# Attention stepped twice as often between projections, six output projections in two pieces, and a conditional whose short side comes first

## The chip, the cores and the metric

The kernel runs on one core of a Trainium2 chip. The metric is the device time of one execution in microseconds, the median of several runs. PE is TensorE, DVE VectorE, ACT ScalarE, POOL GpSimd and SP the engine that issues most DMAs. The names in the order lists below are those of the program (`bank_67` is one of eight PSUM banks).

## What is computed

Two blocks in float32 on 256 tokens of width 1024. The first adds 16 meta tokens and has a pool mixer, a gated linear attention and a hierarchical mixture of 16 experts. The second has two layers, each with a feed-forward part, an attention and another feed-forward part, modulated by a condition. Its stream x (256 tokens) is attended together with a context of 256 tokens; the last layer computes the context only as far as x needs it. One layer of the second block, cut to its core:

```python
u = modulate(rms_norm(h))                 # x and context, per stream
q, k, v = split(u @ w_in)                 # 16 heads of 64
a = window_attention(q_a, k_a, v_a)       # 6 heads, with a sink per head
b = global_attention(rms(q_b), rms(k_b), v_b)   # 4 heads
c = neighbourhood_attention(q_c, k_c, v_c)      # 6 heads, with a bias
h = h + gate * (concat(a, b, c) @ w_out)
```

The mixture of experts has for each token a group (of 4) and two experts in it:

```python
h = silu(xt @ w_gate[e]) * (xt @ w_up[e])
y = y + combine[:, e:e + 1] * (h @ w_down[e])
```

## The kernel before

Every product of two float32 matrices is made from three: each operand is split into a high part (a cast, ACT, "hi") and the rest (a subtraction, DVE, "lo"), and PE multiplies hi by hi, hi by lo and lo by hi. A weight tile of 128 by 1024 comes by DMA into `raw`, ACT makes `hi`, DVE makes `lo`. Tokens stand in the free dimension: x in columns 0 to 255, context in 256 to 511.

One program is written out in Python, and what stands behind what on an engine is decided while it is written. `Program.work(cols)` is called behind each group of matmuls of a projection and counts their columns. At 3000 (`unit`) it calls `tick()`: that prepares the next weight tile (`pump`) and advances every background generator in `bg` by one step. Three matmuls of 512 columns are 1536 columns, so a tick comes every 6 of them (every 12 of 256). The norms, the tails of the projections (rotary embedding, norms of q and k) and the attention of the second block are such generators.

`mix(l)` is the attention part of layer l. Its projections are units in the order of `mix_units(l)`: q and k tiles ("q", 0 to 12; 0 to 7 are queries, 8 to 12 keys), the values of windows and global heads ("vwg", two pieces, `v_units`), the values of the neighbourhood ("vc", four pieces). `attention()` works on items: for each of 8 head pairs two row tiles of x (16 items "x") and, in layer 0, one of the context (8 items "c"). An item may begin when what stands in its `need` is in `have`, until now the query tile, the key tile and the values. One turn of its loop handles three items at different stages, with a `yield` between the stages:

- `t_out` of the item before last: ACT casts the transposed probabilities (`ptH`), DVE makes the rest (`ptL`);
- `exps` (ACT) and `sums` (DVE: sums, reciprocals) of the item before;
- `scores` of a new item (PE, L875), then `maxes` (DVE);
- `v_out` (ACT, DVE) and `values` (PE, L968; L975 broadcasts the reciprocals to all rows);
- `transposes` of the item before (PE, L936).

The generator is started behind the projection "vwg" (`self.start(att)` in `mix`), and advanced by ticks alone. When the projections have run out while items are left, `until` and `drain` advance it with nothing in between.

The output projection has 8 tiles of rows. `OUT2` is ((0, 5), (5, 3)): the first `NO` tiles are made in two pieces, k-tiles 0 to 4 as soon as these heads are done, 5 to 7 later; each piece ends in its own residual addition on DVE (`residual`: h = h + gate * bank). The others are made whole. In layer 0 the last four units of that list (`NW`) run through `run_halves`: first all four on the context's columns, then all four on x; when the context half is done, `after(1)` starts the context's norm for the next feed-forward part, which is advanced by the ticks of the x half. The norm: a sum of squares on PE (L449), a power on POOL, a broadcast on PE (L453), products (DVE, `tmp<-h,modT,bank`), casts (ACT, `uH`), rests (DVE, `uL`). The next part begins with the context's columns.

In the first block, experts have a fixed number of places; a flag (`over`) says whether a second pass is needed. `more_places` loads the flag (L1727) and wraps this pass in `tc.If(rv > 0)` (L1730), which in these runs isn't taken. Its body has 662 instructions on PE, 244 on DVE, 252 on ACT. If it isn't taken, each engine still has to add to its semaphores what the body would have added, in an else side that is placed behind the body; there an engine waits for its own work first.

Small tiles: `small` holds 6 of 128 by 16 for norms, and `sums` 6 of 128 by 16 for the items' maxima, sums and reciprocals.

## Time and profile before

| | us |
|---|---|
| median of 3 runs | 2073.07 (2070.8 to 2075.65) |
| the profiled execution, its own time | 2073.52 |
| its span in the profile | 2071.7 |
| PE busy | 2016.8 (97%) |
| DVE busy | 1406.7 (68%) |
| ACT busy | 818.8 (40%) |

Layer 0's attention part ends at about 946 us, layer 1's at about 1866; the conditional is at 296 to 305 us. A row of the timeline gives the start, the duration, engine, line, operation, output and inputs, sizes and the number of instructions, and in brackets how long the engine was idle before it and what released it. The duration of a matmul row runs past the start of the next one, since matmuls are pipelined; the time that it costs PE is read from start to start.

### The profile page before, as it was taken

What the parts mean: (1) busy time and instruction counts of PE and PEld (TensorE: products, weight loads), DVE (VectorE), ACT (ScalarE), POOL (GpSimd) and SP (SyncE); (2) the same over time, 40 slices, a digit from 0 to 9 for tenths busy, and PEclk for the clock granted to TensorE, in tenths of its full rate; (3) what the DMA queues carried; (4) which work ended last, traced back from release to release, by engine and by line L of the source; (5) the groups of instructions that cost most, each with busy time, mean ns of one, the idle gap of its engine ahead of it and who ended that gap; (6) DMA issues with size and microseconds to landing.
All of it is one profiled execution on the core that took longest, in us unless ns stands there. A gap on an engine that the chain in (4) does not pass through costs nothing.

```text
span 2071.7 us, 30268 instructions
## 1 busy us (share of the span) xinstructions
PE 2016.8 (97%) x11972; PEld 1753.5 (85%) x11972; DVE 1406.7 (68%) x2344; ACT 818.8 (40%) x1404; POOL 64.0 (3%) x87
## 2 busy tenths in 40 slices
PE   7999989999999999999999999999999999999998
PEld 7977769888888988789888888988888899889998
DVE  6888876787763656667886744778665365667554
ACT  5357654222222455555312222432222245555442
POOL 1200000000000100000000000000000010000000
PEclk9999999999999999999999999999999999999999
DMA  6669973565540311025655533365543122137551
GB/s 229 202 241 353 360 258 122 183 203 193 189 126 21 101 57 43 29 89 184 212 186 193 168 109 110 106 210 186 167 164 123 52 68 87 49 105 256 184 175 48
DMA packets 92598, 318.11 MB, mean 154 GB/s; under 512 B 11616, under 2 KB 14976, under 8 KB 92064
## 3 DMA queue, kind: packets, MB, share of 16 engines
q1 hardware_dynamic: 88496, 306.75, 44.5%
q0 software_dynamic: 2624, 9.08, 1.3%
q8 instruction: 96, 1.57, 0.3%
q10 hardware_dynamic: 1328, 0.27, 0.1%
q14 instruction: 54, 0.44, 0.1%
HBM read 315.01 MB, written 1.05 MB: 153 GB/s over the span
## 4 chain that ended last, share of the span: by engine, by line
PE 69%; issue 12%; DVE 3%; ACT 1%; DMA 0%; POOL 0%; POOLq 0%; DVEq 0%; ACTq 0%
PE bank L352 61%; PE bank L968 2%; PE bank L830 2%; PE bank L875 1%; PE bank L936 1%; DVE tmp L130 1%; PE bank L975 1%; ACT probs L912 0%; DVE uL L130 0%; DMA bias<-in_bias_dram 0%; DVE lo L130 0%; ACT ptH L701 0%; PE bank L1785 0%; DVE ptL L130 0%; PE bank L453 0%
## 5 line engine op out<-in xcount | busy, mean ns | idle before, releaser
L352 PE MATMUL bank<-uH,hi 128*128 128x512 f32 (+2 forms) x888 | 301.5, 345 | 7.9 <-DVEq L1730 6.4
L352 PE MATMUL bank<-uH,lo 128*128 128x512 f32 (+2 forms) x888 | 297.7, 341 | 1.5 <-DVE lo L130 1.5
L352 PE MATMUL bank<-uH,xhi 128*128 128x512 f32 (+2 forms) x832 | 285.2, 344 | 2.0 <-ACT uH L1162 2.0
L352 PE MATMUL bank<-uH,xlo 128*128 128x512 f32 (+2 forms) x832 | 283.9, 343 | 0.0
L352 PE MATMUL bank<-uL,hi 128*128 128x512 f32 (+2 forms) x888 | 282.4, 340 | 0.0
L352 PE MATMUL bank<-uL,xhi 128*128 128x512 f32 (+2 forms) x832 | 278.6, 342 | 0.0
L130 DVE CUSTOM_DVE_ANT_0 tmp<-xraw,cs,vec 128x1024 bf16<-128x1024 f32 x192 | 245.8, 1281 | 3.4
L352 PEld LDWEIGHTS bank<-uH,hi 128*128 128x128 f32 x888 | 170.6, 192 | 30.6 <-DVEq L1730 6.9
L352 PEld LDWEIGHTS bank<-uH,lo 128*128 128x128 f32 x888 | 170.6, 192 | 20.0 <-DVE lo L130 1.9
L604 ACT CAST hidH<-tmp 128x512 fp32r<-128x512 f32 (+1 forms) x97 | 51.6, 532 | 335.6 <-DVE tmp L130 335.5
L352 PEld LDWEIGHTS bank<-uH,xhi 128*128 128x128 f32 x832 | 157.8, 190 | 22.6 <-ACT uH L1162 2.4
L352 PEld LDWEIGHTS bank<-uL,hi 128*128 128x128 f32 x888 | 161.4, 191 | 17.1
L352 PEld LDWEIGHTS bank<-uH,xlo 128*128 128x128 f32 x832 | 157.7, 190 | 19.5
L352 PEld LDWEIGHTS bank<-uL,xhi 128*128 128x128 f32 x832 | 154.9, 189 | 19.3
L130 DVE SCALAR_TENSOR_TENSOR h<-bank,modT,h 128x256 f32<-128x256 f32 x204 | 92.8, 480 | 112.9 <-PE bank L352 112.7
L130 DVE TENSOR_TENSOR lo<-raw,hi 128x1024 fp32r<-128x1024 f32 (+3 forms) x111 | 123.7, 1120 | 39.6 <-ACT hi L257 37.9
L130 DVE TENSOR_TENSOR xlo<-xraw,xhi 128x1024 fp32r<-128x1024 f32 (+1 forms) x97 | 115.2, 1189 | 48.7 <-ACT xhi L257 48.5
L595 ACT ACTIVATE tmp<-bank 128x512 f32<-128x512 f32 (+1 forms) x97 | 49.5, 510 | 234.4 <-PE bank L352 232.6
L130 DVE TENSOR_TENSOR tmp<-tmp,bank 128x512 f32<-128x512 f32 (+1 forms) x97 | 55.9, 577 | 126.9 <-PE bank L352 126.2
L130 DVE TENSOR_TENSOR lo<-xraw,hi 128x1024 fp32r<-128x1024 f32 (+1 forms) x96 | 114.9, 1202 | 37.9 <-ACT hi L257 37.5
L352 PE MATMUL bank<-hidH,xhi 128*128 128x512 f32 (+1 forms) x400 | 134.7, 337 | 0.0
L352 PE MATMUL bank<-hidH,xlo 128*128 128x512 f32 (+1 forms) x400 | 134.5, 336 | 0.0
(427 smaller groups left out, 4437.1 us busy)
## 6 DMA issues: line engine op xcount, KB each, us to landing
xraw<-in_w_ada_dram SPq DMA_DIRECT2D x96, 512.0 KB, 3.5
xraw<-in_w_ffn_up_dram SPq DMA_DIRECT2D x52, 512.0 KB, 4.2
xraw<-in_w_ffn_gate_dram SPq DMA_DIRECT2D x50, 512.0 KB, 3.7
raw<-in_w_ada_dram SPq DMA_DIRECT2D x48, 512.0 KB, 4.3
xraw<-in_w_expert_gu_dram SPq DMA_DIRECT2D x43, 512.0 KB, 5.8
raw<-in_w_ffn_gate_dram SPq DMA_DIRECT2D x38, 512.0 KB, 4.3
raw<-in_w_ffn_up_dram SPq DMA_DIRECT2D x36, 512.0 KB, 3.7
xraw<-in_w_ffn_down_dram SPq DMA_DIRECT2D x32, 512.0 KB, 4.0
```

The lines of the kernel that those rows point to most:

```text
L130: return f(*args, **kw)
L352: nc.tensor.matmul(o, a(k), b[:, k, cols], start=start and k == ks[0] and j == 0, stop=stop and k == ks[-1] and j == len(prods) - 1, skip_ ...
L595: nc.scalar.activation(t[:, :cols.stop - cols.start], u.bank[:, cols], AF.Silu)
L604: nc.scalar.copy(H, tt)
L830: nc.tensor.matmul(b, x[:, kk, tok], y(k), start=first, stop=a == ws - 1 and k == per - 1 and j == 2, skip_group_check=True)
L875: nc.tensor.matmul(it["S"][j][:, o], a[rows, i, q], b[rows, kt, kk], start=n == 0 and o.start == 0, stop=n == 2, skip_group_check=True)
L936: nc.tensor.transpose(b[:, o * P:(o + 1) * P], src, self.ident)
L968: nc.tensor.matmul(b[:n, X], a[:, k + dk, v0:v0 + n], p[:, k, :], start=j == 0 and k == ks[0], stop=j == 2 and k == ks[-1], skip_group_che ...
L975: nc.tensor.matmul(b[64 * j:64 * j + 64, 256 + a * P:256 + (a + 1) * P], rs.to_broadcast([P, 64]), self.ident, start=True, stop=True, skip ...
```

## The change

1. `work` advances one generator, the attention (`fast`), also when 1500 columns (`FU`) have been counted since it last moved. With three matmuls of 512 it now moves behind every three, with those of 256 behind every six; all other generators still move at ticks.
2. The attention is started in front of the projection "vwg" instead of behind it. The items of the first five head pairs no longer need "vwg" to begin; `values` yields until it is there. In layer 1 the units 1 and 9 move ahead of "vwg", and 5 behind "vc".
3. `NO` is (6, 6) instead of (4, 4).
4. Maxima and sums use the tiles of `small` (8 now), put back right behind `sums`; the reciprocals go to slices of a new tile `recs`.
5. The flag is loaded ahead of the last expert's down projection, and the conditional gets `preferred_fallthrough_block=False`.

```diff
-NO = (4, 4)
+NO = (6, 6)
+FU = 1500
@@ work
         self.cols += cols
+        self.fast_cols += cols
         if self.cols >= self.unit:
             self.tick()
+        elif self.fast_cols >= FU and self.fast in self.bg:
+            self.fast_cols = 0
+            self.step(self.fast)
@@ mix_units
-        return q(8, 10, 11, 12, 0) + vwg + q(1, 2, 9, 3, 4, 5) + vc + q(6, 7)
+        return q(8, 10, 11, 12, 0, 1, 9) + vwg + q(2, 3, 4) + vc + q(5, 6, 7)
@@ attention
-            st = it["st"] = self.sums.get()
+            st = it["st"] = self.small.get()
...
+            it["rec"] = self.recs.get()
...
-            self.v.reciprocal(st[:, 4:4 + n], st[:, 4:4 + n])
+            self.v.reciprocal(it["rec"][:, :n], st[:, 4:4 + n])
+            self.small.put(st)
...
+            while "vwg" not in self.have:
+                yield
@@ att_items
-        need = lambda i: [i, (8, 8, 8, 9, 9, 10, 11, 12)[i], "vwg" if i < 5 else "vc"]
+        need = lambda i: [i, (8, 8, 8, 9, 9, 10, 11, 12)[i]] + ["vc"] * (i > 4)
@@ mix
+                self.fast = self.start(att)
                 self.v_units("vwg", 2, 0, 256, 4)
                 n += 2
-                self.start(att)
@@ experts
+            if e == E:
+                self.rv = nc.values_load(self.over[0:1, 0:1], min_val=0, max_val=1)
             down(e - 1)
@@ more_places
-        rv = nc.values_load(self.over[0:1, 0:1], min_val=0, max_val=1)
+        rv = self.rv
-        with self.tc.If(rv > 0):
+        with self.tc.If(rv > 0, preferred_fallthrough_block=False):
```

PE in layer 0's attention, in the part that is at 834 to 864 us in the trace of before: transposes (`ident,probs`), scores (`kH,hidH`), values (`ptH,vH`) and transposes follow one another.

```order
L936 MATMUL bank_67<-ident,probs_5938 128x128 x4
L936 MATMUL bank_68<-ident,probs_5938 128x128 x4
L875 MATMUL bank_65<-kH,hidH 128x512
L875 MATMUL bank_63<-kH,hidH 128x512
L875 MATMUL bank_65<-kL,hidH 128x512
L875 MATMUL bank_63<-kL,hidH 128x512
L875 MATMUL bank_65<-kH,hidL 128x512
L875 MATMUL bank_63<-kH,hidL 128x512
L968 MATMUL bank_66<-ptH_5942,vH 128x256 x4
L968 MATMUL bank_66<-ptH_5942,vL 128x256 x4
L968 MATMUL bank_66<-ptL_5943,vH 128x256 x4
L936 MATMUL bank_70<-ident,probs_5939 128x128 x4
```

The same engine in the changed kernel, at a like place of the same attention; the line numbers are 6 to 10 higher, and `uH,hi` and so on are a projection's matmuls.

```order
L978 MATMUL bank_65<-ptH_5944,vH 128x256 x4
L978 MATMUL bank_65<-ptH_5944,vL 128x256 x4
L978 MATMUL bank_65<-ptL_5945,vH 128x256 x4
L358 MATMUL bank_68<-uH,hi_90 128x512
L358 MATMUL bank_68<-uL,hi_90 128x512
L358 MATMUL bank_68<-uH,lo_91 128x512
L944 MATMUL bank_67<-ident,probs_5941 128x128 x4
L944 MATMUL bank_63<-ident,probs_5941 128x128 x4
```

Before, no projection stood between the steps in this part; now three matmuls of 512 columns stand between any two steps of layer 0's attention. In layer 1 some 40 rows of steps without projections are left, about half.

PE at the end of layer 0's attention part, before: the broadcast of the context's norm (`ident,sm`), then matmuls of the x half of the last four output projections, 36 in all, then the first of the next feed-forward part (`uH`).

```order
L453 MATMUL bank_65<-ident,sm_99 128x128 x2
L352 MATMUL bank_70<-hidH,vH 128x256
L352 MATMUL bank_70<-hidL,vH 128x256
L352 MATMUL bank_70<-hidH,vL 128x256
...
L352 MATMUL bank_63<-hidH,ptL_5941 128x256
L352 MATMUL bank_66<-uH,hi_90 128x256
L352 MATMUL bank_66<-uH,lo_91 128x256
```

After (`ones,ssq` and `ones,tmp` are the sums of x's norm):

```order
L459 MATMUL bank_63<-ident,sm_106 128x128 x2
L358 MATMUL bank_67<-hidH,ptH_5944 128x256
L358 MATMUL bank_67<-hidL,ptH_5944 128x256
L358 MATMUL bank_67<-hidH,ptL_5945 128x256
...
L358 MATMUL bank_67<-hidH,ptL_5945 128x256
L455 MATMUL bank_68<-ones,ssq 128x1
L455 MATMUL bank_68<-ones,tmp_94 128x1
...
L358 MATMUL bank_69<-uH,hi_88 128x256
L358 MATMUL bank_69<-uH,lo_89 128x256
```

Of the last four units of layer 0 two are now second pieces of three k-tiles, so the x half has 66 matmuls instead of 96: 6 matmuls are left between the broadcast and the next part, and the sums of x's norm, which stood 24 matmuls behind the next part's beginning, stand in front of it.

DVE at the conditional, before:

```order
L130 TENSOR_TENSOR hTL<-bank_67,hTH 128x256
L130 TENSOR_TENSOR lo_93<-xraw_1173,hi_92 128x1024
L130 TENSOR_TENSOR yL<-bank_69,yH 128x512
L130 TENSOR_TENSOR yL<-bank_63,yH 128x512
L1727 TENSOR_LOAD overi
L1730 COMPARE_AND_BRANCH
L130 TENSOR_TENSOR cw<-rw_1269,rsel 128x2x4 x4
```

After:

```order
L131 TENSOR_TENSOR hTL<-bank_67,hTH 128x256
L1712 TENSOR_LOAD overi
L131 TENSOR_TENSOR lo_93<-xraw_1175,hi_92 128x1024
L131 TENSOR_TENSOR yL<-bank_69,yH 128x512
L131 TENSOR_TENSOR yL<-bank_63,yH 128x512
L1742 COMPARE_AND_BRANCH
L1742 UNCONDITIONAL_BRANCH
```

Before, the body (`cw` is its first row) followed the compare, which jumped over it to the else side. Now the else side, a wait for the engine's own work and the semaphores, follows the compare, and an unconditional jump behind it leads over the body.

## Rows read from the trace of the kernel before

**Rows 1.** The page, busy time of PE over the span.

```profile
PE 2016.8 (97%) x11972; PEld 1753.5 (85%) x11972; DVE 1406.7 (68%) x2344; ACT 818.8 (40%) x1404; POOL 64.0 (3%) x87
```

**Rows 2.** Stretches: length, busy PE, PEld, DVE, ACT, POOL, clock, DMA share, GB/s.

```profile
305.00:326.00 21.00, 20.88 (x128) 20.46 (x129) 10.13 (x18) 5.08 (x8) 1.39 (x2) 0.72 0.26 80
720.00:834.00 114.00, 112.30 (x756) 94.25 (x755) 64.77 (x146) 56.57 (x148) 6.11 (x5) 1.00 0.14 45
834.00:864.00 30.00, 25.35 (x215) 20.12 (x213) 21.49 (x46) 20.82 (x58) 2.21 (x4) 1.00 0.08 25
...
888.00:914.00 26.00, 23.50 (x201) 19.88 (x200) 15.61 (x34) 16.04 (x49) 0.00 (x0) 0.94 0.09 32
...
1797.00:1823.00 26.00, 22.52 (x165) 18.15 (x165) 18.15 (x42) 17.17 (x43) 3.22 (x6) 0.93 0.12 37
```

**Rows 3.** Timeline of layer 0's attention without projections, PE.

```profile
840.83 0.74 PE L968 MATMUL bank<-ptH,vH 128*128 128x256 f32 x4 [1.57 <-ACT ptH L701]
```

**Rows 4.** Timeline of PE, 885 to 893 us, for the steps' prices.

```profile
885.38 0.50 PE L875 MATMUL bank<-kH,hidH 64*128 64x512 f32 x2
...
886.27 0.50 PE L352 MATMUL bank<-hidH,hi 128*128 128x512 f32 x1
...
887.75 0.64 PE L968 MATMUL bank<-ptH,vH 128*128 128x256 f32 x4
...
889.18 1.03 PE L936 MATMUL bank<-ident,probs 128*128 128x128 f32 x8
889.98 0.72 PE L968 MATMUL bank<-ptH,vH 128*64 128x256 f32 x4
...
892.17 0.39 PE L875 MATMUL bank<-kH,hidH 64*128 64x256 f32 x2
```

**Rows 5.** Waits of PE, 720 to 834 us: total, times, longest.

```profile
PE bank L936 <- DVE vL L130: 1.5, 1, 1.5
```

**Rows 6.** Groups of DVE, 720 to 914 us: busy, mean ns; idle before, releaser.

```profile
L130 DVE TENSOR_TENSOR lo<-raw,hi 128x1024 fp32r<-128x1024 f32 x6 | 7.3, 1220 | 0.3 <-ACT hi L257 0.3
L130 DVE TENSOR_TENSOR hidL<-raw,hidH 128x256 fp32r<-128x256 f32 x17 | 7.2, 425 | 8.0 <-ACT hidH L701 8.0
...
L130 DVE TENSOR_TENSOR sums<-sums 128x2 f32<-128x2 f32 x6 | 1.0, 161 | 11.6 <-ACT sums L917 11.6
```

**Rows 7.** Timeline, all engines, end of layer 0's attention part.

```profile
939.84 0.48 DVE L130 SCALAR_TENSOR_TENSOR h<-bank,modT,h 128x256 f32<-128x256 f32 x1 [1.36 <-PE bank L352]
940.41 0.42 ACT L429 ACTIVATE tmp<-h 128x256 f32<-128x256 f32 x1 [2.87 <-DVE h L130]
941.06 0.61 PE L453 MATMUL bank<-ident,sm 128*128 128x128 f32 x4
...
941.71 2.44 DVE L130 SCALAR_TENSOR_TENSOR tmp<-h,modT,bank 128x256 f32<-128x256 f32 x6 [1.05 <-PE bank L453]
...
942.22 2.51 ACT L505 ACTIVATE uH<-tmp,modT 128x256 fp32r<-128x256 f32 x6 [1.39 <-DVE tmp L130]
```

**Rows 8.** Stretches, end of layer 1's attention part, columns as in the second group.

```profile
1866.00:1870.30 4.30, 1.76 (x12) 1.49 (x12) 2.69 (x7) 1.84 (x4) 0.71 (x1) 0.94 0.92 349
1870.30:1874.00 3.70, 3.63 (x20) 3.63 (x21) 3.70 (x10) 3.70 (x10) 0.00 (x0) 0.61 0.89 357
```

**Rows 9.** Timeline around the conditional, PE and DVE.

```profile
299.57 1.28 DVE L130 TENSOR_TENSOR yL<-bank,yH 128x512 fp32r<-128x512 f32 x2
...
305.11 0.58 PE L352 MATMUL bank<-uH,hi 128*128 128x256 f32 x1 [6.45 <-DVEq L1730]
305.28 1.28 DVE L130 CUSTOM_DVE_ANT_0 tmp<-raw,cs,vec 128x1024 bf16<-128x1024 f32 x1 [4.43 <-DVEq L1730]
...
312.29 1.88 DVE L130 TENSOR_TENSOR h<-h,bank 128x512 f32<-128x512 f32 x3 [1.48 <-PE bank L1611]
```

**Rows 10.** Instructions of the conditional's line: duration ns, first and last start.

```profile
L1730 PEldq COMPARE_BRANCH  x1: 3952/3952/3952, 296.7 to 296.7; - x1
...
L1730 DVEq COMPARE_BRANCH  x1: 72/72/72, 300.0 to 300.0; - x1
```

More of the change, by code (lines that the diff above doesn't have):

```diff
@@ L145, in __init__ @@
         self.bg = []
+        self.fast, self.fast_cols = None, 0
         self.v = Vector(self, tc.nc.vector)
@@ L152, in tick @@
         self.now += self.cols / CK if self.cols else 1.3
-        self.cols = 0
+        self.cols = self.fast_cols = 0
         self.pump()
@@ L972, in values @@
                     for j in range(2):
-                        c = 4 + j if it["k"] == "x" else 4 + 2 * j + a
-                        rs = it["its"][a if it["k"] == "x" else 0]["st"][:, c:c + 1]
+                        c = j if it["k"] == "x" else 2 * j + a
+                        rs = it["its"][a if it["k"] == "x" else 0]["rec"][:, c:c + 1]
                         nc.tensor.matmul(b[64 * j:64 * j + 64, 256 + a * P:256 + (a + 1) * P], rs.to_broadcast([P, 64]),
@@ L988, in v_out @@
             for o in it["its"]:
-                self.sums.put(o["st"])
+                self.recs.put(o["rec"])
             self.y_left[i] -= 2 if it["k"] == "x" else 1
@@ L2011, in build @@
             self.ssq = t("ssq", [P, 512])
-            self.small = Free([t(f"sm{i}", [P, 16]) for i in range(6)])
+            self.small = Free([t(f"sm{i}", [P, 16]) for i in range(8)])
             self.ones = t("ones", [P, 1])
@@ L2062, in mix @@
                     self.rot = t("rot", [P, P], F32R)
-                    self.sums = Free([t(f"sums{i}", [P, 16]) for i in range(6)])
                     rot32 = self.raw2.q[0][:, :P]
@@ L2066, in mix @@
                     self.ind = t("ind", [P, 2])
+                    recs = t("recs", [P, 24])
+                    self.recs = Free([recs[:, 4 * i:4 * i + 4] for i in range(6)])
                     for d, n in ((rot32, "rot"), (self.cos, "cos"), (self.sin, "sin"), (self.ind, "ind")):
```

## The prediction

> **What bounds the kernel now.** I read the page first, then the table of stretches, then the timeline and the waits in the stretches where something is lost. TensorE (PE) works for 2016.8 us, 97% of the span [rows 1], so whatever the change gains has to come out of the 55 us in which PE does nothing, out of moments at half clock, or out of work removed. No matmul work is removed: the same columns run before and after. The table of stretches [rows 2] shows where PE loses time in the parts that the change touches. At 720 to 834 us, where steps of layer 0's attention alternate with projections, it is idle for 114.00 − 112.30 = 1.70 us of 114. At 834 to 864 us it is idle for 30.00 − 25.35 = 4.65 us, at 888 to 914 for 2.50 us at a granted clock of 0.94, and in layer 1, at 1797 to 1823, for 3.48 us at 0.93. In those three stretches the attention steps stand back to back, since the projections have run out.
>
> The timeline shows why they are slow there [rows 3]: the values wait 1.57 us for ScalarE's cast of the transposed tile. The chain of scores, maxima (VectorE), exponentials (ScalarE), transposes, casts (ScalarE, VectorE) and values is longer than what PE has in between. With projections between the steps (720 to 834) the same chain hides.
>
> **Part 1: attention stepped per 1500 columns, started before the values' projection.** The order lists show the effect: in layer 0 no attention steps stand back to back any more; three matmuls of 512 columns always lie between two steps. In layer 1 about half of the back-to-back part is left.
>
> What is to be recovered in layer 0: 4.65 + 2.50 us idle, and the half clock of 888 to 914. A mean of 0.94 there means that 12% of 26 us ran at half rate, 3.1 us, of which half is lost: 1.56 us. Busy time overstates PE a little, since a row's duration runs past the start of the next (the transposes at 889.18 say 1.03 us, and the next row starts 0.80 us later [rows 4]); for some five waits that hides 5 × 0.2 = 1.0 us more. Sum: 9.7 us.
>
> In layer 1: 3.48 us idle, 14% of 26 us at half rate (half of 3.6 us, 1.8 us), and about 0.3 of the same overlap, 5.6 us; half of the bare stretch stays, so 2.8 us.
>
> What is added: the items start earlier, but values now wait for "vwg". So the first of them come right behind the last matmul of that projection, when ScalarE and VectorE still have to move its banks into vH and vL. Such a wait happens once in the trace: transposes held 1.5 us by vL [rows 5]. I take 1.5 us for each layer, bounds 0 (the filler matmuls cover it) and 3.0 (vH's share in front of vL's as well).
>
> Does the filler really hide the chain at the doubled pace? PE's work for one pair of row tiles of a head pair, read from start to start [rows 4]: scores 0.89 (885.38 to 886.27), transposes 0.80 (889.18 to 889.98), values 1.43 (887.75 to 889.18) and 2.19 (889.98 to 892.17, with the broadcast of the sums). Two scores, two transposes, both values: 7.0 us. Between them stand seven steps of three matmuls, each half of the six between 886.27 and 887.75, 0.74 us: 5.2 us. So a pair takes PE about 12.2 us, 6.1 us per item. The bare chain took 30 us for the six items of 834 to 864, 5.0 us each, with VectorE busy for 21.49 / 6 = 3.6 us of it [rows 2]. The filler brings VectorE work of its own: 3.5 steps are 10.5 matmuls, 0.44 of the 24 of a weight tile, and a tile costs one subtraction of 1.22 us, about five rotary steps of 0.42 [rows 6] and one twice as wide (the split of the context's columns, 0.7 as an estimate), 4.0 us, so 1.8 us per item. VectorE then has 5.4 of 6.1 us: it fits, but densely. I take 1 us per layer 0 for collisions (bounds 0, and the third rival below).
>
> **Part 2: six of eight output projections in two pieces.** Matmuls stay; two more residual additions per layer and stream, four in layer 0 and two in layer 1, of about 0.48 us (the row at 939.84 [rows 7]), run on VectorE beside PE's work (it is busy 15.61 of 26 us even in the bare stretch), at no cost while PE has projections queued. Without that cover they would cost 6 × 0.48 = 2.9 us. Two more weight pieces and their DMAs per layer go through SP's queue, in a stretch where the DMA engines are busy for 0.08 to 0.14 [rows 2]: nothing.
>
> But the edit has a side effect that the diff does not show. Layer 0 ends with the last four units of the list run in two halves, first the context columns, then x, and the context's norm is made under the x half. Before, these four were whole projections (96 matmuls of 256 in the x half). Now two of them are second pieces of three k-tiles, so that half has 66. The order list shows what that does: 36 matmuls used to stand between the broadcast of the context's norm and the first matmul of the next FFN, now there are 6, and the norm sums of x follow them at once. The chain behind the broadcast is in the trace [rows 7]: broadcast at 941.06, VectorE's six products 941.71 to 944.15, the last residual addition (0.48) now queued behind them, to 944.6; ScalarE's six casts end at 944.73, its square of 0.42 follows, and the sums can start at about 945.25, 4.2 us behind the broadcast. PE has some 0.4 us for the broadcast and 6 × 0.123 = 0.74 us of matmuls (half of 0.247, the six of 512 above): 3.1 us idle. Layer 1's end already looks like this [rows 8]: 4.30 − 1.76 = 2.5 us idle, then a clock of 0.61 for 3.7 us, so 2.9 us at half rate, half of it lost, 1.4 us. I take 3.1 + 0.9 = 4.0 us as a loss, the clock at two thirds, since this gap is one and not three pieces (bounds: 0, if the queue runs in a luckier order, and the 30 × 0.123 = 3.7 us of cover removed plus 1.4, 5.1).
>
> **Part 3: the jump.** At the conditional of the expert overflow PE is idle for 6.45 us, up to 305.11, "released" by VectorE's queue [rows 9], and the stretch behind it runs at 0.72 [rows 2]. PE's own compare takes 3.95 us [rows 10]; VectorE ends its last work at 299.57 + 1.28 = 300.85 and starts again at 305.28, so its jump takes about 4.4 us. Before, each engine jumps over the body and then signals. Now it waits for its own work, signals, and then jumps. PE would do so at about 298.7, be free at 298.7 + 3.95 = 302.7, and find VectorE's signal there since 300.9: 2.4 us sooner than now. VectorE starts no sooner, and waited only 1.48 us for PE at 312.29 [rows 9], so beyond that it becomes the bound. I take 2 us (bounds: a loss of 0.8 us, if VectorE's jump starts late by what its compare was ahead, 300.85 − 300.0, and a gain of 8.4). The earlier load of the flag is one of 0.5 us on queues that run ahead: nothing.
>
> What a jump costs decides here. The rows show a compare of 0.07 us on VectorE but no work for 4.4 us behind it [rows 9, 10], so I charge the distance. The Trainium skill, "Runtime: NRT & Kernel Launch", section "Instruction fetch mechanics", says that a taken branch to a target outside the fetched pages stalls for the fetch; by that the unconditional jump over the body pays as the compare did. "Advanced Engine Details and Errata", section "Control Flow Timing", gives about 51 ns for a branch that is always taken; by that alone the jump would be free. The trace has no such jump over a body.
>
> **Part 4: small tiles.** The sums use `small`, returned at once, and the reciprocals go to `recs`. Same instructions, two more buffers for the norms: nothing.
>
> **The sum.** Layer 0: 9.7 − 1.5 − 1.0 − 4.0 = 3.2. Layer 1: 2.8 − 1.5 = 1.3. Jump: 2. Together 6.5 us. Against the profiled run of 2073.52 us, 0.45 above the median of 2073.07, that is 2067.0; against the median 2066.6. I say 2067.
>
> **Rivals.** A, the jump is nearly free: then VectorE too goes on at 301 and the whole 6.45 us is gained, with some 2 of the 5.9 us that a clock of 0.72 costs in 21 us [rows 2] (56% at half rate, half of that lost), 6.4 us more than charged: 2061. For it: the compares' short rows. Against: PE's own 3.95.
>
> B, new waits take the place of the old: both first values wait the full 3.0 us instead of 1.5 (3.0 more), the seam costs its full 5.1 (1.1 more), the jump gives 1.5: 2071. For it: layer 1's seam shows exactly such waits.
>
> C, slower: at the doubled pace the items' chain does not overlap with the filler's VectorE and ScalarE work, because both queues are in order: a subtraction of the sums waits for ScalarE (11.6 us before the six of them [rows 6]), and the next weights' subtraction stands behind it. Fully serial an item costs 5.0 + 1.8 = 6.8 us instead of 6.1; two thirds of that 0.7 us on all 24 items of layer 0 is 11 us, the seam with B's terms 1 more: 2079. It turns the result into a loss from 6.5 / 24 = 0.27 us per item. Against it: at half that pace, between 720 and 834 us, PE waits only 1.7 us.
>
> D, the change does not do what it says: the order lists exclude it for the steps.
>
> **Chances.** Forecast 0.55 (its own range 2063 to 2071, its terms at either bound in part), A 0.10, B 0.17, C 0.18. 0.2% is 4.1 us, about what a measurement of this kernel can tell from no change, so below 2068.9 counts as faster. Of the forecast 0.44 lies there, and all of A: 0.54. B and the rest of the forecast are within: 0.28. C is slower: 0.18. The range goes from 2058, past A's price, to 2078, close to C's; it leaves out the worse half of C and the better part of A, about 0.15.
>
> **What would show it.** Right: no waits of L936 on ScalarE between 820 and 870 us, the first values behind vwg waiting 1 to 2 us, about 3 us idle and a half-clock moment at the start of layer 0's second FFN, PE restarting about 4 us after its last expert matmul and VectorE 4 us after its own. Wrong: transposes that wait in every loop of layer 0 (C), a restart of both engines within 1 us (A), or no gap at the seam.

## The result, and the profile after

The changed kernel takes 2091.81 us (median of 4 runs, 2088.28 to 2092.80) against 2073.35 us before: a ratio of 1.0086, interval 1.0069 to 1.0104. I had said 2067, in a range of 2058 to 2078. It is 18.5 us slower, beyond the end of the range, and on the other side.

The page of the changed kernel:

```profile
span 2090.6 us, 30234 instructions
...
PE 2018.8 (97%) x11942; PEld 1760.3 (84%) x11942; DVE 1410.1 (67%) x2354; ACT 821.0 (39%) x1408; POOL 63.7 (3%) x87
```

The share of PE is as it was [rows 1], so the page alone says nothing. The stretches do (columns as in [rows 2]: length, busy PE, PEld, DVE, ACT, POOL, clock, DMA share, GB/s). Layer 0's attention and output projections are the first three rows, the end of that part and the start of the second feed-forward part the next three, layer 1's attention and its end the last four:

```profile
780.00:830.00 50.00, 45.70 (x286) 38.09 (x286) 29.67 (x57) 21.88 (x49) 2.46 (x1) 0.97 0.16 52
830.00:880.00 50.00, 50.00 (x345) 39.30 (x343) 30.46 (x71) 28.55 (x74) 5.43 (x10) 1.00 0.16 50
880.00:906.00 26.00, 25.34 (x189) 20.38 (x188) 16.58 (x34) 13.61 (x43) 0.00 (x0) 1.00 0.09 25
...
940.00:960.00 20.00, 19.06 (x133) 18.68 (x134) 17.58 (x36) 13.69 (x22) 0.81 (x1) 0.83 0.41 135
960.00:1000.00 40.00, 40.00 (x257) 36.58 (x256) 8.64 (x15) 8.22 (x15) 0.00 (x0) 1.00 0.19 65
1000.00:1034.00 34.00, 23.84 (x88) 18.05 (x87) 23.15 (x33) 7.09 (x9) 0.00 (x0) 0.85 0.43 139
...
1800.00:1830.00 30.00, 25.72 (x173) 21.25 (x173) 17.30 (x40) 14.17 (x36) 2.21 (x4) 0.83 0.15 51
1830.00:1855.00 25.00, 24.93 (x209) 22.04 (x207) 17.18 (x40) 14.76 (x35) 3.22 (x6) 1.00 0.17 52
1855.00:1875.00 20.00, 14.77 (x94) 13.57 (x93) 11.60 (x23) 8.57 (x17) 0.00 (x0) 0.79 0.38 119
1875.00:1895.00 20.00, 15.71 (x106) 15.12 (x105) 12.76 (x26) 10.86 (x18) 0.71 (x1) 0.78 0.59 209
```

What I had hoped for is there: from 830 to 906 PE hardly stops, where before 4.65 us were idle in 30 and 2.50 in 26 [rows 2]. What I had not looked for is the row of 1000 to 1034: 10.2 us idle and half-clock moments behind them, in a feed-forward part that had no idle time before. In the row ahead of it VectorE works for 8.64 us of 40; the kernel before, in the same 40 us:

```profile
960.00:1000.00 40.00, 40.00 (x266) 36.79 (x265) 33.98 (x53) 16.41 (x23) 0.00 (x0) 1.00 0.64 200
```

To see where time comes and goes, I cut all traces at the same points: rows of ScalarE's gate activations (the first and the last of layer 0's first feed-forward part, the eleventh of its second, the last of layer 1's first, and in layer 1's second the load of the function's table, 1.3 us ahead of the first) and the last values matmul of each attention. The table has the lengths before in us and, for the changed kernel, the differences. Each column is one profiled execution; over all runs of this document such an execution lies up to 2.8 us from the median of its kernel.

| stage | before | after |
|---|---|---|
| to the conditional | 295.7 | −0.5 |
| conditional and layer 0's first feed-forward part | 345.9 | −6.1 |
| layer 0's attention, to its last values | 270.4 | +0.5 |
| rest of its projections, start of the next part | 120.4 | +17.3 |
| feed-forward parts up to layer 1's attention | 613.1 | −8.9 |
| layer 1's attention, to its last values | 200.7 | +5.5 |
| rest of its projections, to the first gate | 29.8 | +9.1 |
| last feed-forward part and end | 195.7 | +1.9 |
| span | 2071.7 | +18.9 |

Two things stand out that are no part of the prediction: 17 us lost in the fourth row, and 15 us gained in the second and the fifth row, most of it in feed-forward parts that the change doesn't touch. Layer 1 loses 14.6 us, where I had forecast a gain of 1.3.

**The starvation.** Around 1000 us the timeline of the changed kernel (start, duration, engine, instruction, idle time before and releaser) reads, first the loads of weights in SP's queue:

```profile
977.66 0.33 SPq L245 DMA_DIRECT2D xraw<-in_w_ada_dram  x1
1005.36 0.33 SPq L245 DMA_DIRECT2D raw<-in_w_ffn_gate_dram  x1
```

then the compute engines:

```profile
1002.11 0.69 DVE L131 TENSOR_TENSOR tmp<-tmp,bank 128x512 f32<-128x512 f32 x1 [8.81 <-PE bank L358]
1002.72 1.28 DVE L131 CUSTOM_DVE_ANT_0 tmp<-raw,cs,vec 128x1024 bf16<-128x1024 f32 x1
...
1008.83 1.04 ACT L263 CAST xhi<-raw 128x1024 fp32r<-128x1024 f32 x1 [5.38 <-DMA raw<-in_w_ffn_gate_dram]
...
1009.93 0.80 PE L358 MATMUL bank<-uH,xhi 128*128 128x512 f32 x1 [7.92 <-ACT xhi L263]
```

PE waits for a weight tile that ScalarE casts as soon as its DMA has landed, and that DMA was issued at 1005.36, 27.7 us behind the one before it. In between SP's queue had no buffer to load into: the loads before it were tiles of `in_w_ada`, the modulation weights, and VectorE read the first of them only at 1002.72, though it had been idle for 8.81 us before 1002.11. In the kernel before, VectorE does this work from 969.80 on:

```profile
969.80 1.28 DVE L130 CUSTOM_DVE_ANT_0 tmp<-raw,cs,vec 128x1024 bf16<-128x1024 f32 x1
```

So VectorE was free, the tiles were there, and the instruction simply stood too late in its queue.

What puts it there is the planner's `pump`, code that the diff doesn't touch:

```python
if due or (self.p_ada < self.ada_to and self.here(self.p_ada, MA)
           and self.dve < self.now + MD and self.tmps.q):
    self.ada_next()
```

`self.dve` is an account of VectorE's backlog that every VectorE instruction raises; `self.now` is a clock that ticks advance, by the columns of projections or, when there are none, by 1.3 per tick. Attention's own matmuls are in no tick's columns. Before, the attention cost ticks of its own, and the bare steps above all advanced the clock. With the steps between the ticks, the account goes on and the clock stands: when the second feed-forward part fetches its first weights, the account is 1 to 2 ahead of the clock in the kernel before and about 36 ahead in the changed one (both in the planner's microseconds, from the program and not from a trace). Modulation work isn't emitted until they meet again, or until a weight that is needed next finds no buffer to be loaded into.

### The profile page after: what moved, and what is told of

The parts are those of the page before. It is cut to its first block, busy times and chain, and to the rows that moved or that the text cites. A ratio compares the mean times of both kernels' runs of the same rounds, so it can differ in the third digit from the quotient of the medians.

```text
span 2090.6 us, 30234 instructions
## 1 busy us (share of the span) xinstructions
PE 2018.8 (97%) x11942; PEld 1760.3 (84%) x11942; DVE 1410.1 (67%) x2354; ACT 821.0 (39%) x1408; POOL 63.7 (3%) x87
## 4 chain that ended last, share of the span: by engine, by line
PE 80%; DVE 3%; ACT 2%; issue 1%; DMA 0%; POOL 0%; POOLq 0%; DVEq 0%; ACTq 0%
PE bank L358 69%; PE bank L978 3%; PE bank L836 3%; PE bank L881 2%; PE bank L944 2%; DVE tmp L131 1%; PE bank L985 1%; DVE uL L131 0%; PE bank L459 0%; ACT ptH L707 0%; ACT probs L918 0%; DVE h L131 0%; DVE lo L131 0%; DVE ssq L131 0%; ACT hi L263 0%
## 5 line engine op out<-in xcount | busy, mean ns | idle before, releaser
L358 PE MATMUL bank<-uH,xhi 128*128 128x512 f32 (+2 forms) x864 | 297.0, 344 | 11.7 <-ACT xhi L263 9.6
L358 PE MATMUL bank<-uH,xlo 128*128 128x512 f32 (+2 forms) x864 | 295.8, 343 | 0.6 <-DVE xlo L131 0.5
L358 PE MATMUL bank<-uL,xhi 128*128 128x512 f32 (+2 forms) x864 | 292.9, 342 | 0.0
L358 PE MATMUL bank<-uL,hi 128*128 128x512 f32 (+2 forms) x872 | 272.0, 338 | 0.0
L358 PEld LDWEIGHTS bank<-uH,xhi 128*128 128x128 f32 x864 | 165.5, 191 | 31.7 <-ACT xhi L263 10.4
L358 PEld LDWEIGHTS bank<-uH,xlo 128*128 128x128 f32 x864 | 165.2, 191 | 19.9 <-DVE xlo L131 1.7
L358 PEld LDWEIGHTS bank<-uL,xhi 128*128 128x128 f32 x864 | 164.2, 191 | 18.4
L358 PEld LDWEIGHTS bank<-uL,hi 128*128 128x128 f32 x872 | 157.3, 192 | 17.3 <-issue 1.9
L358 PE MATMUL bank<-hidH,xhi 128*128 128x512 f32 (+1 forms) x430 | 144.3, 336 | 0.0
L358 PE MATMUL bank<-hidL,xhi 128*128 128x512 f32 (+1 forms) x430 | 144.2, 335 | 0.0
L358 PE MATMUL bank<-hidH,xlo 128*128 128x512 f32 (+1 forms) x430 | 144.2, 335 | 0.0
```

The lines of the kernel that those rows point to most:

```text
L358: nc.tensor.matmul(o, a(k), b[:, k, cols], start=start and k == ks[0] and j == 0, stop=stop and k == ks[-1] and j == len(prods) - 1, skip_ ...
```

## The experiments

All times are medians; each ratio is against runs of the kernel before on the same chip, whose medians were 2072.5 to 2073.3 us. The stages of each are in the table at the end of this section.

**1. The account set back.**

```diff
         self.drain(att)
+        self.dve = min(self.dve, self.now)
```

> The changed kernel with one line more: when the attention of a layer is done, the planner's account of VectorE's backlog is set back to its own clock. Theory 1: the 10 us of idle TensorE at the start of layer 0's second feed-forward part, and the slow clock behind it (together some 13.7 us against the kernel before), come from that account. Attention steps no longer come in ticks of their own, so the planner's clock stands while the account of VectorE grows (36 us ahead), the modulation weights are put off, keep all raw tiles, and the next weights can't be loaded. It expects about 2079 us, no wait of TensorE of over 2 us between 960 and 1060 us, and modulation work of VectorE there from the start. Rival: the starvation comes from the loads themselves (two more weight pieces, a later queue); then this line changes nothing: 2092 us and the same wait.

Measured: 2073.56 us, ratio 1.0007 (0.9997 to 1.0016); 18 us less than the changed kernel, and more than I had put on it. The same stretches as above:

```profile
960.00:1000.00 40.00, 40.00 (x252) 36.31 (x252) 34.37 (x50) 13.79 (x20) 0.00 (x0) 1.00 0.61 203
1000.00:1034.00 34.00, 34.00 (x152) 28.15 (x151) 25.70 (x38) 10.37 (x13) 0.00 (x0) 1.00 0.67 226
```

PE is busy throughout at full clock, VectorE works for 34 of the 40 us (8.6 in the changed kernel), and the DMA share is 0.61 instead of 0.19. That is theory 1. One line of bookkeeping decides over 18 us.

**2. Four split projections.**

```diff
-NO = (6, 6)
+NO = (4, 4)
```

> The changed kernel with 4 instead of 6 output projections in two pieces, as before. Theory 2: the short pieces cost twice. They shorten the cover of the context's norm at the end of layer 0 (3.7 us), and in layer 1 a piece of three k-tiles is 2304 columns while one weight tile is prepared per 3000, so the stock runs dry (four waits of 1.0 to 1.6 us and a slow clock, some 8 us with what follows). It expects about 2081 us, no wait for ptL or vL in the output projections of layer 1, the starvation in layer 0's second feed-forward part unchanged (8 to 10 us idle). Rival: layer 1's stock runs dry because fewer ticks come while the attention runs, not because of the pieces; then only the 3.7 us come back, 2088 us, and the waits in layer 1 stay.

Measured: 2084.77 us, 1.0059 (1.0042 to 1.0075), 7 us less than the changed kernel. The starvation stays, as expected (that stage is 14.8 us longer than before, 17.3 in the changed kernel). But layer 1 loses 10.8 instead of 14.6 us, so the pieces explain a quarter of it, and the rival was half right: something else empties the stock there.

**3. The conditional alone.**

```diff
+            if e == E:
+                self.rv = nc.values_load(self.over[0:1, 0:1], min_val=0, max_val=1)
             down(e - 1)
...
-        with self.tc.If(rv > 0):
+        with self.tc.If(rv > 0, preferred_fallthrough_block=False):
```

> The kernel before with only the conditional changed (flag loaded ahead of the last down projection, short side first). Theory 3 (as predicted): TensorE starts about 2.4 us sooner, 2071 us, and VectorE starts no sooner. Rival A: the jump is free, 8 us, 2065 us. Rival: the matmul pitch of the feed-forward parts, 231 ns for 512 columns before and 227 ns in the changed kernel, goes with the code's place; then it is 227 ns here too, and some 12 us more are gained: 2059 us.

Measured: 2070.93 us, 0.9995 (0.9986 to 1.0005): 1.6 us, too small to be told from no change. PE restarts like this:

```profile
300.15 0.39 PE L352 MATMUL bank<-uH,hi 128*128 128x256 f32 x1 [3.69 <-issue]
303.67 0.37 PE L352 MATMUL bank<-uH,hi 128*128 128x256 f32 x1 [1.84 <-issue]
```

and VectorE like this:

```profile
301.94 1.28 DVE L130 CUSTOM_DVE_ANT_0 tmp<-raw,cs,vec 128x1024 bf16<-128x1024 f32 x1 [3.29 <-issue]
```

The compare and its jump no longer wait for another engine ("issue" instead of DVEq), and PE is idle for 3.69 us instead of 6.45 [rows 9], then, 3.5 us later, for another 1.84. That second gap isn't in the kernel before, so PE loses 5.5 us instead of 6.45: 0.9 us less. The jump over the body is paid: rival A is out. By the Trainium skill, "Runtime: NRT & Kernel Launch", section "Instruction fetch mechanics", a taken jump to code that isn't fetched stalls. The 3.69 us agree; the 1.84 us may be the next piece of code, which no run here shows by itself.

With 512 columns and the lent weight tiles `xhi` and `xlo`, the matmuls keep their old pace here, 232 ns from start to start. So the last rival of that expectation, that the pace goes with the code's place, is out too.

**4. Six split projections alone.**

```diff
-NO = (4, 4)
+NO = (6, 6)
```

> The kernel before with only the 6 split output projections. Theory 2: the seam of layer 0 costs 3.7 us and layer 1's output projections wait for weights, but with the stock that the bare attention steps build up less than in the changed kernel: 2079 us. Rival: without the faster steps the pieces cost only the seam, 2077 us, or pay for themselves by filling layer 0's end, 2071 us. The modulation work isn't put off here (the account is 1 us ahead), so no starvation in layer 0's second feed-forward part.

Measured: 2086.64 us, 1.0070 (1.0053 to 1.0087): 14 us, twice what I expected. PE's waits (total, times, longest) at the end of layer 0's part and the start of the next:

```profile
PE bank L449 <- DVE ssq L130: 3.7, 1, 3.7
PE bank L352 <- DVE vL L130: 1.3, 1, 1.3
PE bank L352 <- DVE xlo L130: 1.1, 1, 1.1
```

and at layer 1's end:

```profile
PE bank L352 <- DVE vL L130: 3.0, 2, 1.8
PE bank L453 <- POOL sm L411: 2.2, 1, 2.2
```

The first row of all is the seam that the prediction had derived from the order list, 3.7 us (3.1 forecast). The rows for `vL` are weight tiles in lent buffers whose rests come too late, in both layers. That the short pieces use up weight tiles faster than one is prepared per tick fits them and the planner's code; it was not tried by itself.

**5. The faster steps alone.**

```diff
+FU = 1500
...
+        self.fast_cols += cols
         if self.cols >= self.unit:
             self.tick()
+        elif self.fast_cols >= FU and self.fast in self.bg:
+            self.fast_cols = 0
+            self.step(self.fast)
...
-                self.start(att)
+                self.fast = self.start(att)
```

> The kernel before with only the attention stepped per 1500 columns (started behind vwg, 4 split output projections). The planner's account of VectorE is 13 us ahead at the end of layer 0's attention here, 36 in the changed kernel. Theory 1 expects the bare stretches of attention filled (up to 10 us), but modulation work still put off at the start of layer 0's second feed-forward part, at a third of the price (4 us), and no seam: about 2068 us. Rival C of the prediction: the chain of the items doesn't overlap with the filler's work; then attention gains nothing in either layer and the time is 2075 us or more.

Measured: 2087.55 us, 1.0074 (1.0057 to 1.0091). Theory 1's number (2068) was wrong: no starvation at all in the next part (−0.4 us there), but 8.9 us more in layer 0's attention, 6.3 us more at layer 1's end. Attention gains nothing, as rival C had it, though by another way: with the start behind the values' projection there are still 148 attention rows without projections between them in the order list (276 before, 40 in the changed kernel), and PE idles 14.9 us in that stage against 10.3. Why these rows are worse than those of before I did not settle.

**6. The changed kernel without the faster steps.**

```diff
-FU = 1500
+FU = 10 ** 9
```

> The changed kernel without the steps per 1500 columns. Theory 1: without them the account of VectorE is 1 us ahead, so the starvation is gone; what stays is the price of 6 split output projections (14 us in the run that had them alone), less 12 us for the place of the tiles and 2 us for the conditional: 2072 us. Rival: the early start of the attention costs or gains by itself; then it differs from that by more than 3 us.

Measured: 2074.41 us, 1.0010 (1.0000 to 1.0020): 17 us less than the changed kernel, and no starvation. It is within 3 us of the sum that theory 1 gave.

**7. Four split, the account set back.** The changed kernel with the edits of 1 and 2.

> The changed kernel with 4 split output projections and the planner's account set back behind the attention. Theory 2, if the prices add: 2073.6 us (account set back, 6 split) less the 14 us that 6 split projections cost alone, 2060 us. Rival: the split costs only 7 us beside the faster steps, as the run with 4 split projections and no set-back showed: 2066 us. Against the kernel before with 8 small tiles it tells what the faster steps are worth in all.

Measured: 2066.68 us, 0.9970 (0.9957 to 0.9982). The rival's number: beside the faster steps, the six split projections cost 7 us, not 14. In the stages (7 against 1) that is 3.2 us in layer 0 and 2.2 in layer 1.

**8. The place of the tiles.** While comparing traces I saw that the feed-forward parts with 512 columns, which the change doesn't touch, run 1.5% faster in the changed kernel. The matmuls with the weight tiles `xhi` and `xlo` do: 232.5 ns from start to start before, 226.5 ns after; those with `hi` and `lo` have 227 ns in both. `small` with two tiles more moves everything allocated behind it by 128 bytes. Two more tiles alone don't fit into the kernel before, beside `sums`. So the kernel before, with nothing but this, which moves `xhi`, `xlo` and the raw tiles lent with them:

```diff
             def extra(fx, limit, n=4, hl=5):
+                fx.tile([P, 32], F32, name="pad")
```

> The kernel before with an unused tile of 128 bytes per partition in front of the lent weight tiles of each feed-forward part (8 small tiles did not fit beside the sums tiles). Nothing else moves: xhi and xlo lie 128 bytes higher, as in the changed kernel (address modulo 256 is 192 instead of 64; hi, lo and uH are at 192 in all kernels). Theory 4: 226 to 227 ns between matmuls of 512 columns with xhi and xlo, 12 us less: 2061 us. Rival: the pitch goes with something else in the change; 232 ns and 2073 us.

Measured: 2060.54 us, 0.9946 (0.9930 to 0.9963), 12.0 us less, as expected. 230 us of a feed-forward part (columns as above), first before, then with the pad: 1001 matmuls of 512 columns and 1016, some 60% of them with `xhi` and `xlo`.

```profile
1030.00:1260.00 230.00, 230.00 (x1001) 188.00 (x1000) 150.93 (x219) 55.38 (x68) 0.00 (x0) 1.00 0.49 159
```

```profile
1030.00:1260.00 230.00, 230.00 (x1016) 190.51 (x1015) 147.89 (x213) 56.31 (x69) 0.00 (x0) 1.00 0.47 157
```

In single rows, two of before and two with the pad; between the starts lie 0.24 and 0.23 us in the first, 0.22 and 0.23 in the second:

```profile
1150.02 0.40 PE L352 MATMUL bank<-uH,xlo 128*128 128x512 f32 x1
1150.26 0.40 PE L352 MATMUL bank<-uH,xhi 128*128 128x512 f32 x1
1150.49 0.39 PE L352 MATMUL bank<-uL,xhi 128*128 128x512 f32 x1
```

```profile
1149.93 0.39 PE L352 MATMUL bank<-uH,xlo 128*128 128x512 f32 x1
1150.15 0.39 PE L352 MATMUL bank<-uH,xhi 128*128 128x512 f32 x1
1150.38 0.39 PE L352 MATMUL bank<-uL,xhi 128*128 128x512 f32 x1
```

**9. The place and the conditional.** The edits of 8 and 3 on the kernel before.

> The kernel before with the 128 bytes and the changed conditional. If both prices add (12 us and 2 us): 2059 us, and faster than both kernels. Rival: the conditional's gain is used up by the faster feed-forward part behind it: 2061 us.

Measured: 2057.02 us, 0.9926 (0.9909 to 0.9942): faster than both kernels. Beside the pad the conditional is worth 3.5 us by the medians (of four runs each, whose ranges don't meet). The two profiled executions show less: 1.1 us in the span, 0.2 of it in the conditional's stage, where PE is idle for 4.01 + 1.84 us instead of 5.58.

**10. The early start alone.** The changed kernel without the faster steps and with four split projections (edits of 2 and 6).

> The changed kernel without the steps per 1500 columns and with 4 split output projections: the kernel before with the early start of the attention, the other order of units in layer 1, the place of the tiles and the conditional. Theory: the early start alone is worth little, the items only wait elsewhere; 2059 us as for the place and the conditional alone, within 3 us. Rival: the early start pays by itself (fewer bare steps), 2055 us; or it is what costs (first values waiting behind vwg), 2064 us. The run with the faster steps beside it (4 split, account set back) took 2066.7 us; the difference is what the faster steps cost at this place.

Measured: 2061.87 us, 0.9955 (0.9938 to 0.9971). 4.9 us above experiment 9, but its runs spread from 2059.1 to 2064.4 and its profiled span is only 0.9 us longer. The early start costs something between 1 and 5 us and gains nothing: 266 bare rows are left of 276, and layer 0's attention is 3.0 us longer than before. One more thing differs from experiment 9 here: with the larger `small`, the attention part's own tiles lie 128 bytes further too. The 561 matmuls of 256 columns with its lent weight tiles come every 119.8 ns instead of 118.6, 0.7 us in all; what it does to attention's own matmuls was not tried.

**11. Ticks given back.** Experiment 7 and, behind layer 1's attention,

```diff
+        if not both:
+            for _ in range(3):
+                self.tick()
```

> The changed kernel with 4 split output projections, the account set back and three empty ticks of the planner behind layer 1's attention. Theory 5: the faster steps take from the planner the ticks in which it prepares weights ahead while the attention ends; the stock at layer 1's second pieces is 2 tiles instead of 3 and falls to 0, and TensorE waits there for the rests of weight tiles (vL 1.8 us, ptL 1.5). With 4 in stock these waits go: 2066.7 − 4 = 2063 us. Rival: the waits are VectorE's own backlog, whatever is in stock; then they stay, 2067 us.

Measured: 2062.29 us, 0.9950 (0.9934 to 0.9967). PE's waits at layer 1's end, in experiment 7 and here:

```profile
PE bank L358 <- DVE vL L131: 1.8, 1, 1.8
PE bank L358 <- DVE ptL L131: 1.5, 3, 1.1
PE bank L459 <- POOL sm L417: 1.1, 1, 1.1
```

```profile
PE bank L459 <- POOL sm L417: 1.1, 1, 1.1
...
PE bank L358 <- DVE vL L131: 0.2, 1, 0.2
```

The waits for weight tiles are gone but for 0.2 us, and the stage is back at its old length (+0.1 us). Theory 5 holds: bare attention steps had cost ticks, and ticks prepare weights.

**12. The place, by width.** Experiment 9 without the pad in the last feed-forward part.

```diff
-            def extra(fx, limit, n=4, hl=5):
-                fx.tile([P, 32], F32, name="pad")
+            def extra(fx, limit, n=4, hl=5, pad=32):
+                if pad:
+                    fx.tile([P, pad], F32, name="pad")
...
-                extra(fx, limits[2])
+                extra(fx, limits[2], pad=0)
```

> As the run with the 128 bytes and the conditional (2057 us), but without the 128 bytes in the last feed-forward part, which has x's 256 columns only. In the traces the same tiles xhi and xlo take 232.5 ns per matmul of 512 columns at the old place and 226.5 at the new one, but 118.7 ns per matmul of 256 at the old place and 120.0 at the new one. If the place acts through the number of columns, the last part gains back 1.3 ns on about 950 matmuls, 1.2 us, with what else differs there up to 2: 2055.5 us. Rival: the 118.7 ns were an effect of the run; then 2057 us and 120 ns.

Measured: 2055.75 us, 0.9914 (0.9897 to 0.9930): 17.6 us less than the kernel before, the fastest version tried. The interval overlaps that of experiment 9, so the matmuls have to show it. Over 130 us of the last part, which has 256 columns only, 1085 matmuls run with the pad (experiment 9, first) and 1094 without:

```profile
1900.00:2030.00 130.00, 130.00 (x1085) 130.00 (x1085) 72.14 (x92) 53.83 (x74) 0.00 (x0) 1.00 0.46 153
```

```profile
1900.00:2030.00 130.00, 130.00 (x1094) 130.00 (x1093) 72.56 (x92) 54.29 (x75) 0.00 (x0) 1.00 0.47 151
```

Cut as above, the last feed-forward part is 2.1 us longer than before in experiment 9 and 0.2 us here.

The stages of the runs (numbers of the experiments; A is the changed kernel), us against the kernel before. Stages that an edit doesn't touch still differ between two executions, layer 1's attention by 1.7 us in experiment 3 and the time ahead of the conditional, which is left out here, by 2.7 us in experiment 5; a single difference of that size proves little.

| stage | A | 1 | 2 | 4 | 5 | 6 | 7 | 8 | 9 | 10 | 11 |
|---|---|---|---|---|---|---|---|---|---|---|---|
| conditional, first part | −6.1 | −6.0 | −6.1 | 0.0 | −1.6 | −6.3 | −6.3 | −5.8 | −6.0 | −6.3 | −6.1 |
| layer 0's attention | +0.5 | +0.5 | +0.1 | +6.4 | +8.9 | +9.7 | +0.1 | +0.9 | −0.1 | +3.0 | −0.5 |
| its end, next start | +17.3 | +2.1 | +14.8 | +0.6 | −0.4 | 0.0 | −0.7 | −1.4 | −0.8 | −0.5 | −1.2 |
| feed-forward parts | −8.9 | −8.7 | −9.2 | −0.5 | +0.6 | −8.7 | −8.2 | −8.2 | −8.2 | −8.2 | −8.2 |
| layer 1's attention | +5.5 | +2.5 | +5.6 | +2.0 | −0.3 | +2.3 | +2.6 | −1.6 | −1.8 | −1.4 | +3.8 |
| its end | +9.1 | +6.2 | +5.2 | +2.8 | +6.3 | +2.0 | +3.9 | 0.0 | 0.0 | +0.1 | +0.1 |

Six split projections move work from the third row into the second, ahead of the last values matmul, so their price in layer 0 is the sum of both rows: 7.0 us in experiment 4, 7.2 in 6 against 10.

## Why the prediction was wrong

The runs form a chain from the kernel before to the changed one. Their differences, each run against its own runs of the kernel before, add up to the result by construction (the sum before rounding); what a part is worth depends on its place in the chain, as the six split projections show (14.1 us alone, 6.2 here).

| part | from | us |
|---|---|---|
| 128 bytes | 8 | −12.0 |
| conditional | 9 less 8 | −3.5 |
| early start, order of units | 10 less 9 | +4.9 |
| faster steps, the planner's account | 2 less 7 | +18.6 |
| faster steps, ticks missing in layer 1 | 7 less 11 | +3.8 |
| faster steps, the rest | 11 less 10 | +0.4 |
| six split projections | A less 2 | +6.2 |
| sum | | +18.5 |

**The step that failed** is in part 1: "What is to be recovered in layer 0", and its neighbour for layer 1. It costed the attention steps as instructions on engines, and the projections between them as cover, and never asked what else the steps had done in the program: they had been ticks, and ticks advance the planner's clock and prepare weights. Both were known ahead of the prediction ("At 3000 (`unit`) it calls `tick()`"), and the order list of VectorE would have shown the modulation work further back: behind the products of the context's norm, eight weight subtractions come ahead of the first modulation row in the changed kernel's trace, five in the one before. I compared the orders only at the places that I had costed. This was put at nothing and cost 18.6 + 3.8 = 22.4 us. None of my rivals has this mechanism; C came out on the right side by another one.

The terms that were priced failed as well. By the chain they come to 4.9 (early start) + 0.4 (faster steps, the rest) + 6.2 (six split projections) − 3.5 (conditional) = +8.0 us, where the forecast had 3.0 − 11.5 + 4.0 − 2.0 = −6.5. The largest miss among them is the recovery itself: 9.7 + 2.8 − 1.0 = 11.5 us forecast, none measured. Without the planner's part and without the 12.0 us that the place of the tiles gave by luck, the changed kernel would by this count still have been slower.

**Layer 0's attention.** 9.7 us of stalls were to be recovered, less 2.5. Idle time in that stage fell from 10.3 to 6.2 us only: the bare waits went, others came at the faster pace (1.88 us for a norm of queries, 1.82 for ScalarE's exponentials, 0.59 for the cast of a query tile), and a half-clock moment with them (0.97 over 50 us). Beside the early start alone, the faster steps gain 2.9 us there (7 against 10); but the early start had made the stage 3.0 us longer, so that it ends no shorter than before (+0.1 in experiment 7, +0.5 in the changed kernel). Why the early start does that stays open. The row that I took as proof of cover, 112.30 us busy of 114 at half the pace, could not show it.

**The first values behind vwg** were charged 1.5 us per layer. No run isolates them. In the changed kernel's trace no wait of PE in either attention names vH or vL, and the 1.5 us of before [rows 5] is gone, so the term was nothing there; the early start as a whole costs 1 to 5 us by another way.

**The seam.** Its mechanism was right: PE waits for the sums of x's norm, 3.7 us where six split projections stand alone and 2.54 in the changed kernel (3.1 forecast), and a slow clock follows (0.83 over 20 us, 3.4 us lost; 0.9 forecast). But the split was costed at nothing in layer 1, and it costs 2.2 us there (experiment 1 against 7), with PE waiting for weight tiles.

**Layer 1** was to gain 1.3 us and loses 14.6 in the changed kernel. A part comes back with the account (5.9 us, experiment 1), 2 to 4 with four split projections, 3.8 with the ticks; some 4 us in its attention stay with the faster steps (experiment 11, +3.8, waits of 3.7 us for the exponentials against 1.0 in experiment 9). That looks like the chain of the items at a pace that it can't hold, rival C's mechanism in layer 1, where projections have 256 columns. Shown is the wait; that the pace or C's queue order causes it was not tried.

**The conditional.** 2 us forecast, 1.6 measured alone (within the noise), 3.5 beside the pad. PE's first gap shrank by 2.8 us in experiment 3 (2.4 forecast), but a second one of 1.84 us, which I had not charged, took most of that back. VectorE restarted after 3.3 to 4.5 us, as said.

**The small tiles** were put at "nothing". They were worth 12 us, the largest gain of the change, by their place alone, and that gain was luck.

## What to carry to other kernels

Where a program plans its own order, a change of pace is a change of the planner's inputs: compare the order on all engines to the end of the program, not only where the change is made, and look for work that has moved far from its old neighbours. When a stage that an edit doesn't touch gets faster or slower, look at addresses: 128 unused bytes were worth more than everything that was planned. And cut two traces at the same landmarks before explaining a sum, since here −15.5 and +34 us stood behind +18.5.

## What the runs showed of the hardware

- Matmuls of 512 columns with weights at an address of 64 modulo 256 bytes within the partition follow one another every 232.5 ns (228 to 241, uneven); at 192 every 226.5 ns (even). The moving tiles stand at 192 in both. With 256 columns it is the other way round: 118.7 ns (115 to 122, uneven) at 64, 120.0 ns (even) at 192 (experiments 8 and 12). Other addresses were not tried, and why it is so was not settled; the duration of the weight load rows is 188 ns in both.
- A jump over the body of a conditional (662 instructions on PE) cost microseconds. Where the unconditional jump took it, PE was idle for 3.5 to 4.1 us before its next matmul and for another 1.7 to 2.0 us some 3 us later, in all ten traces that have it. Where the compare itself jumped (the kernel before and experiments 4, 5 and 8), its row lasts 4.0 to 5.8 us and PE was idle for 5.6 to 6.5 us in one piece, the end of it waiting for VectorE.
- A gap of 7.9 us in PE's work (1002.0 to 1009.9) was followed by half-clock moments: 0.86 over the next 24 us, 3.4 us lost. With the 10.2 us of idle time between 1000 and 1034 that makes 13.6 of the 15.2 us by which the stage is longer than in experiment 1:

```profile
1009.93:1034.00 24.07, 21.84 (x79) 16.73 (x80) 19.95 (x28) 5.42 (x7) 0.00 (x0) 0.86 0.54 175
```
